# A hybrid decoder block on one core: the order of two of the seven products, and a fourth pair by seven products in the second part's down groups

## The chip, the cores and the metric

The kernel runs on one core of one Trainium2 chip. The metric is the device time of one execution in microseconds (us); lower is better. Before the change it is 1952.89 us, the median of three runs (1952.71 to 1953.48).

## What is computed

One decoder block with SEQ = 256 tokens, D_MODEL = 2048, D_FF = 5632, all in fp32:

```python
h = h + 0.5 * swiglu(rms_norm(h, ffn1_norm[i]), ffn1_w_gu[i], ffn1_w_down[i])
h = h + hybrid_mixer(rms_norm(h, mix_norm[i]), w_in[i], ...)
h = h + 0.5 * swiglu(rms_norm(h, ffn2_norm[i]), ffn2_w_gu[i], ffn2_w_down[i])
gate = jax.nn.sigmoid(rms_norm(h, ple_norm[i]) @ ple_w_gate[i])
h = h + gate * (p[i] @ ple_w_proj[i])
...
def swiglu(x, w_gu, w_down):
    gate, up = jnp.split(x @ w_gu, 2, axis=-1)
    return (jax.nn.silu(gate) * up) @ w_down
```

The change lies in the two SwiGLUs ("ffn 1" and "ffn 2"). The mixer between them and the gate behind them are not touched.

## The kernel before

**Precision.** Every fp32 operand of a matrix product is split into a high and a low part (`hi`, a rounding cast on ScalarE, ACT; `lo = x - hi`, a subtraction on VectorE, DVE), and a product takes three matmuls of TensorE (PE): hi times hi, hi times lo, lo times hi. One matmul has a 128x128 stationary side (activations) and a 128x512 moving side (weights).

**Groups.** A SwiGLU has 11 column blocks of 512 in its gate and up matrices, cut into three parts of 3, 4 and 4 blocks (`PARTS`, line 28). For each block there is a group `gu` (four banks of PSUM: gate and up, `g` and `u`, for two token tiles each), and behind the blocks of a part there are two groups `dn` for the down product of that part, with 1024 of the 2048 output columns each (four banks `d`). The groups of part 1 (the second part) of ffn 1 are the four `gu` groups from about 219 to 374 us and the two `dn` groups from 374 to 466 us; in ffn 2 they end at 1614 us.

**Pairs and products.** A group's inner dimension comes in pairs, of 256 rows each. A pair done the plain way is loaded as 512 KB for each of the two column blocks (`raw`), split by `weight_pair` (lines 74 and 75: `whi`, `wlo`, three buffers each) and multiplied by 12 matmuls (lines 540 to 542). So a pair takes 24 matmuls for both column blocks. The first `ns` pairs of a group go another way, by the scheme of Strassen and Winograd: the weights are cut into four quarters, loaded as tiles `R` (128 x 512 `ns`), and seven products of combined quarters with combined left sides give the four banks, at 3 matmuls for each pair and product: 21 instead of 24 for each pair. `NS` = 4 pairs in a `gu` group; `NS_DOWN` (line 32) = 2, 3, 3 pairs in the `dn` groups of the three parts.

**The seven products** (`Group.all_sums`, `halved` and `product`, lines 281 to 349). For each product the sum of quarters standing in `R` is split into `shi` (line 295, ACT) and `slo` (line 296, DVE), two buffers each; behind the first products DVE adds other quarters onto `R` (line 304), or GpSimd's queue (POOL) loads a quarter once more with an adding DMA (line 311). The products go into the banks c21, c12, c21, c21, c11, c12, c21 in this order. Behind the first two ACT copies the bank to c11 and c22 (line 344). Behind the third and the fourth ACT copies c21 into a tile `part` (line 347), which DVE subtracts from c12, and from c22 (line 349). The fourth product adds to c21, as the third, so it may start only when the copy of line 347 behind the third is through.

**The left sides** (`halves`, lines 425 to 462). For two pairs at a time DVE adds hi and lo of the activations into a tile `S` (line 452), makes four differences in it (line 458), ACT casts it to `Sh` (line 460), and DVE makes `Sl` (line 461). Products 0, 4 and 6 (counted from 0) take the activations themselves as left side; the others take `Sh` and `Sl`.

**The order.** While a group's plain pairs run, the seven products of the following group are put between them, one behind each plain pair from the first or the third on, and the rest behind the last (`plan`, the list `at`); the loads of the quarters of the group after that are put behind products 4 to 6, into the places that the follower's quarters leave (`loads`). This program order is then moved about by the framework's scheduler, engine by engine, so that a product's matmuls can stand scattered between those of plain pairs. Each engine works its own list strictly in order.

**The last block of a part.** `down_input` (line 477 on) makes `hTh` and `hTl`, the left side of the down product, of a block: two products on DVE, a transposition by 32x32 blocks, DMAs out and in, a cast and a subtraction. The plain pairs of the first `dn` group that use the last block are put last.

Of the kernel before, what the change touches and what calls it, by code (L numbers as in the profile page):

```python
# [10 lines left out]
F32 = mybir.dt.float32  # L11
# [16 lines left out]


NS = 4  # L30
NS_DOWN = tuple(3 if i1 - i0 == 4 else 2 for i0, i1 in PARTS)


W_IN_ORDER = (2, 0, 4, 3, 1, 5, 8, 10, 12, 9, 11, 13, 6, 7)
# [9 lines left out]
def block_kernel(ctx, tc, a, out):  # L44
# [200 lines left out]
    class Group:  # L245
# [32 lines left out]
        def loads(self, last=None):  # L278


            free = [last.home[q] for q in ((0, 1), (1, 0), (1, 1), (0, 0))] if last else ["R0", "R1", "R2", "R3"]
            self.queue = nc.gpsimd if last else nc.sync
            use = (0, 0), (0, 1), (1, 1), (1, 0)
            self.home = dict(zip(use, free))
            return [("load", lambda q=q: self.load(*q)) for q in use]

        def all_sums(self):

            fp = current[0]

            def halved(j, b):
                w = self.raw[j, b]
                hi = fp.tile([P, NS, NB], F32R, tag="shi", name="shi", bufs=2)[:, 0:self.ns]
                lo = fp.tile([P, NS, NB], F32R, tag="slo", name="slo", bufs=2)[:, 0:self.ns]
                keep(nc.scalar.copy(hi, w))  # L295
                nc.vector.tensor_tensor(out=lo, in0=w, in1=hi, op=ALU.subtract)  # L296
                return hi, lo

            def keep(ins):

                return tc.keep_in_program_order(ins) if self.first == "2" else ins

            def add(x, y):
                keep(nc.vector.tensor_tensor(out=self.raw[x], in0=self.raw[x], in1=self.raw[y], op=ALU.add))  # L304

            def add_loaded(x, y):


                if self.first:
                    return add(x, y)  # L310
                nc.gpsimd.dma_start(out=self.raw[x], in_=self.quarters[y[1]][y[0]], accum_op=ALU.add)

            for i, q in enumerate(((0, 0), (0, 0), (0, 0), (0, 1), (1, 0), (1, 1), (0, 0))):
                ws = halved(*q)
                if i == 0:
                    add((0, 0), (0, 1))
                    add_loaded((0, 1), (1, 1))
                elif i == 1:
                    add((0, 0), (1, 1))
                elif i == 2:  # L320
                    add_loaded((0, 0), (1, 0))
                yield ws
# [97 lines left out]
    def halves(kind, his, los, ns, wait=0):  # L420


        for _ in range(wait):
            yield
        fp = current[0]

        sh = fp.tile([P, NS, 2, 2, P], F32R, tag="Sh", name="Sh")
        sl = fp.tile([P, NS, 2, 2, P], F32R, tag="Sl", name="Sl")

        def side(i, g):  # L430
            if i in (0, 4, 6):
                k, t = 2 * (g % 2) + (i > 0), i // 6
                c = slice(t * P, (t + 1) * P)
                return his[g // 2][:, k, c], los[g // 2][:, k, c]
            j, t = {1: (1, 1), 2: (0, 0), 3: (0, 1), 5: (1, 0)}[i]
            return sh[:, g, j, t, :], sl[:, g, j, t, :]

        sides[kind] = side

        for g0 in range(0, ns, 2):  # L440
            n = min(2, ns - g0)
            hi, lo = his[g0 // 2], los[g0 // 2]
            keep = lambda ins: ins
            if g0 and n == 1:

                keep = tc.keep_in_program_order
                yield
            if n == 2:
                x = fp.tile([P, 2 * NB], F32, tag="sil", name="S")
            else:  # L450
                x = act.tile([P, NB], F32, tag="nat", name="S", bufs=4)
            keep(nc.vector.tensor_tensor(out=x, in0=hi[:, 0:2 * n].bitcast(F32).rearrange("p k x -> p (k x)"),
                                         in1=lo[:, 0:2 * n].bitcast(F32).rearrange("p k x -> p (k x)"), op=ALU.add))
            xv = x.rearrange("p (g j t y) -> p g j t y", g=n, j=2, t=2)
            a11, a12, a21, a22 = (xv[:, :, j, t, :] for t in range(2) for j in range(2))
            for o, y, z, op in ((a22, a21, a22, ALU.subtract), (a21, a11, a21, ALU.subtract),
                                (a11, a22, a11, ALU.subtract), (a12, a11, a12, ALU.add)):
                nc.vector.tensor_tensor(out=o, in0=y, in1=z, op=op)
            sx = [y[:, g0:g0 + n].rearrange("p g j t y -> p (g j t y)") for y in (sh, sl)]
            nc.scalar.copy(sx[0], x)  # L460
            nc.vector.tensor_tensor(out=sx[1], in0=x, in1=sx[0], op=ALU.subtract)
            yield

    def ffn(n, nT, r, scale, next_norm, stat):
        xs = picker(*nT)
        late = callable(r)
        with tc.tile_pool(name="ffn", bufs=1) as fp:
# [43 lines left out]
            for group, todo in ffn_plan[n]:  # L511
# [14 lines left out]
                    group.new_banks()  # L526
                for kind, one in todo:
                    if kind == "seventh":
                        group.follower.product(one)
                        continue  # L530
                    b, g = one
                    whi, wlo = next_weights()
# [29 lines left out]
                    else:  # L562
# [7 lines left out]
                        hTl.append(tl)  # L570
                        i0, i1 = PARTS[group.part]

                        last = (3 if i1 - i0 == 4 else 2) if len(hTh) == i1 else 0
                        gen = down_input(outs, sil, th, tl, last)
                        next(gen)

# [801 lines left out]
```

## Time and profile before

| | |
|---|---|
| median of three runs | 1952.89 us (1952.71 to 1953.48) |
| the profiled execution, its own time | 1953.25 us |
| its span in the trace | 1951.5 us |
| PE busy | 1932.7 us, 99% of the span, 8884 matmuls |
| weight loads of PE (beside the matmuls) | 1591.6 us, 82% |
| DVE busy | 1567.9 us, 80% |
| ACT busy | 1163.1 us, 60% |
| POOL busy | 148.8 us, 8% |
| granted clock of TensorE | 0.998 |
| chain that ended last | PE 87%, DVE 6%, DMA 4%, issue 2%, ACT 1% |

A matmul's busy time (0.39 us) is longer than the distance from one start to the next (0.23 us), since matmuls are pipelined; so 99% busy says only that PE seldom stands still. What a matmul costs is the distance of starts. The span is 1.75 us shorter than the execution's own time, which has the launch around it.

### The profile page before, as it was taken

The page shows a single profiled execution, that of the slowest core. Times are in us where ns is not written, and L with a number is a line of the kernel's source. Part 1 is how long each engine was busy: PE and PEld are TensorE (multiplying, and loading weights), DVE is VectorE, ACT ScalarE, POOL GpSimd, SP SyncE. Part 2 cuts the span into 40 slices and gives each one's busy share as a digit, 9 for nine tenths or more (in the row PEclk, how much of TensorE's full clock was granted, in tenths as well). Part 3 has the DMA queues.
Part 4 walks back from the last instruction along what each step waited for, and adds up shares of the span by engine and source line. Part 5 has one row for each costly group of instructions (what it writes and reads, how often), then busy time and mean ns, then how long its engine had stood idle before and what let it go on. Part 6 is the DMA issues. An engine that isn't in the chain of part 4 may idle for free.

```text
span 1951.5 us, 24163 instructions
## 1 busy us (share of the span) xinstructions
PE 1932.7 (99%) x8884; PEld 1591.6 (82%) x8884; DVE 1567.9 (80%) x1679; ACT 1163.1 (60%) x1358; POOL 148.8 (8%) x226
## 2 busy tenths in 40 slices
PE   9999999999999999999999999999999999999997
PEld 7888888888888888878788888888888788887886
DVE  7889878997889766797856579889888987888965
ACT  6656666566665567664555456566565755656653
POOL 0010100000010000010100000010000100001000
PEclk9999999999999999999999999999999999999999
DMA  8778888788887765556565786888898987988864
GB/s 311 268 238 276 255 288 285 227 293 251 282 283 237 225 216 172 175 169 209 173 201 160 244 289 226 226 285 289 241 282 251 303 266 237 272 255 282 249 208 141
DMA packets 144184, 475.06 MB, mean 243 GB/s; under 512 B 19649, under 2 KB 47297, under 8 KB 129857
## 3 DMA queue, kind: packets, MB, share of 16 engines
q1 hardware_dynamic: 107200, 302.16, 44.4%
q0 software_dynamic: 25920, 160.44, 30.2%
q10 hardware_dynamic: 10944, 10.91, 1.7%
q8 instruction: 69, 1.13, 0.2%
q14 instruction: 51, 0.41, 0.1%
HBM read 451.44 MB, written 22.02 MB: 243 GB/s over the span
## 4 chain that ended last, share of the span: by engine, by line
PE 87%; DVE 6%; DMA 4%; issue 2%; ACT 1%; SPq 0%; POOL 0%; POOLq 0%; DVEq 0%; ACTq 0%
PE g L340 5%; PE d L541 5%; PE d L542 5%; PE g L339 5%; PE d L540 4%; PE g L341 4%; PE u L540 4%; PE u L542 4%; PE u L541 4%; PE g L541 4%; PE g L542 4%; PE pj L109 4%; PE pj L110 4%; PE pj L111 4%; PE g L540 4%
## 5 line engine op out<-in xcount | busy, mean ns | idle before, releaser
L74 ACT CAST whi<-raw 128x1024 fp32r<-128x1024 f32 (+1 forms) x489 | 512.1, 1050 | 427.1 <-PE pj L111 109.9
L75 DVE TENSOR_TENSOR wlo<-raw,whi 128x1024 fp32r<-128x1024 f32 (+1 forms) x489 | 592.0, 1217 | 166.1 <-ACT whi L74 163.8
L296 DVE TENSOR_TENSOR slo<-R,shi 128x2048 fp32r<-128x2048 f32 (+2 forms) x224 | 445.2, 1989 | 149.0 <-ACT shi L295 147.6
L295 ACT CAST shi<-R 128x2048 fp32r<-128x2048 f32 (+2 forms) x224 | 374.2, 1671 | 140.5 <-DVE R L304 62.1
L109 PE MATMUL pj<-whi,nTh 128*128 128x512 f32 x448 | 179.4, 401 | 0.0
L110 PE MATMUL pj<-wlo,nTh 128*128 128x512 f32 x448 | 175.3, 391 | 1.1 <-DVE wlo L75 1.1
L111 PE MATMUL pj<-whi,nTl 128*128 128x512 f32 x448 | 174.9, 390 | 0.0
L541 PE MATMUL d<-wlo,hTh 128*128 128x512 f32 x448 | 174.3, 389 | 0.0
L540 PE MATMUL d<-whi,hTh 128*128 128x512 f32 x448 | 174.2, 389 | 0.0
L542 PE MATMUL d<-whi,hTl 128*128 128x512 f32 x448 | 173.7, 389 | 0.0
L541 PE MATMUL g<-wlo,nTh 128*128 128x512 f32 x400 | 155.9, 390 | 0.4 <-DVE wlo L75 0.4
L541 PE MATMUL u<-wlo,nTh 128*128 128x512 f32 x400 | 155.7, 389 | 0.5 <-DVE wlo L75 0.5
L542 PE MATMUL g<-whi,nTl 128*128 128x512 f32 x400 | 155.8, 390 | 0.0
L542 PE MATMUL u<-whi,nTl 128*128 128x512 f32 x400 | 155.7, 389 | 0.0
L540 PE MATMUL g<-whi,nTh 128*128 128x512 f32 x400 | 155.4, 390 | 0.0
L540 PE MATMUL u<-whi,nTh 128*128 128x512 f32 x400 | 154.2, 389 | 0.2 <-ACT whi L74 0.2
L304 DVE TENSOR_TENSOR R<-R 128x2048 f32<-128x2048 f32 (+2 forms) x68 | 135.7, 1995 | 0.1
L110 PEld LDWEIGHTS pj<-wlo,nTh 128*128 128x128 f32 x448 | 84.2, 188 | 18.9 <-DVE wlo L75 2.7
L111 PEld LDWEIGHTS pj<-whi,nTl 128*128 128x128 f32 x448 | 84.1, 188 | 17.6
L542 PEld LDWEIGHTS d<-whi,hTl 128*128 128x128 f32 x448 | 84.1, 188 | 17.6
L541 PEld LDWEIGHTS d<-wlo,hTh 128*128 128x128 f32 x448 | 84.1, 188 | 17.6
L540 PEld LDWEIGHTS d<-whi,hTh 128*128 128x128 f32 x448 | 84.1, 188 | 17.4
(332 smaller groups left out, 3445.2 us busy)
## 6 DMA issues: line engine op xcount, KB each, us to landing
raw<-in_w_gu SPq DMA_DIRECT2D x199, 512.0 KB, 5.7
raw<-in_w_down SPq DMA_DIRECT2D x112, 512.0 KB, 6.5
raw<-in_w_in SPq DMA_DIRECT2D x112, 512.0 KB, 3.4
R<-in_w_gu2q POOLq DMA_DIRECT2D x54, 1024.0 KB, 8.6
R<-in_w_gu1q POOLq DMA_DIRECT2D x48, 1024.0 KB, 8.6
raw<-in_w_out SPq DMA_DIRECT2D x32, 512.0 KB, 4.2
tT<-scr SPq DMA_DIRECT2D x22, 512.0 KB, 5.1
R<-in_w_down11q POOLq DMA_DIRECT2D x12, 768.0 KB, 6.0
```

Source lines behind the costliest of these rows:

```text
L74: nc.scalar.copy(hi[:, j, :], raw[:, j, :])
L75: nc.vector.tensor_tensor(out=lo[:, j, :], in0=raw[:, j, :], in1=hi[:, j, :], op=ALU.subtract)
L109: nc.tensor.matmul(outs[t], xh[:, c], whi[:, j, :], start=st, stop=False)
L110: nc.tensor.matmul(outs[t], xh[:, c], wlo[:, j, :], start=False, stop=False)
L111: nc.tensor.matmul(outs[t], xl[:, c], whi[:, j, :], start=False, stop=sp)
L295: keep(nc.scalar.copy(hi, w))
L296: nc.vector.tensor_tensor(out=lo, in0=w, in1=hi, op=ALU.subtract)
L304: keep(nc.vector.tensor_tensor(out=self.raw[x], in0=self.raw[x], in1=self.raw[y], op=ALU.add))
L339: nc.tensor.matmul(out, xh, whi[:, g, :], start=st, stop=False, skip_group_check=True)
L540: nc.tensor.matmul(out, xh[:, c], whi[:, j, :], start=st, stop=False, skip_group_check=True)
L541: nc.tensor.matmul(out, xh[:, c], wlo[:, j, :], start=False, stop=False, skip_group_check=True)
L542: nc.tensor.matmul(out, xl[:, c], whi[:, j, :], start=False, stop=sp, skip_group_check=True)
```

## The change

Five things are edited; all else stays.

1. `NS_DOWN` becomes (2, 4, 3): the two `dn` groups of the second part take four instead of three pairs by seven products, in both SwiGLUs. Their quarters grow from 128x1536 to 128x2048, and they have four instead of five plain pairs for each column block.
2. `SEVEN` puts product 4 (into c11) in front of product 3 (into c21), in the loads' splits and in the products.
3. `loads` gives the freed tiles of quarters on in the order in which they now come free.
4. `halves` makes the left sides of four pairs of a `dn` group in three steps: pairs 0 and 1 together, pair 2 and pair 3 in tiles of one pair each (128x512, of the pool's `nat`), and doesn't hand over to other work between the last two.
5. `last`, the number of steps for which the last block's cast is put off, is 2 instead of 3 in the second part.

```diff
-NS_DOWN = tuple(3 if i1 - i0 == 4 else 2 for i0, i1 in PARTS)
+NS_DOWN = (2, 4, 3)
+SEVEN = (0, 1, 2, 4, 3, 5, 6)
...
-            free = [last.home[q] for q in ((0, 1), (1, 0), (1, 1), (0, 0))] if last else ["R0", "R1", "R2", "R3"]
+            free = [last.home[q] for q in ((1, 0), (0, 1), (1, 1), (0, 0))] if last else ["R0", "R1", "R2", "R3"]
...
-            for i, q in enumerate(((0, 0), (0, 0), (0, 0), (0, 1), (1, 0), (1, 1), (0, 0))):
-                ws = halved(*q)
+            for i in SEVEN:
+                ws = halved(*((0, 0), (0, 0), (0, 0), (0, 1), (1, 0), (1, 1), (0, 0))[i])
...
-        for g0 in range(0, ns, 2):
-            n = min(2, ns - g0)
-            hi, lo = his[g0 // 2], los[g0 // 2]
+        for g0, n in {1: ((0, 1),), 2: ((0, 2),), 3: ((0, 2), (2, 1)),
+                      4: ((0, 2), (2, 1), (3, 1)) if kind == "dn" else ((0, 2), (2, 2))}[ns]:
+            k0 = 2 * (g0 % 2)
+            hi, lo = (x[g0 // 2][:, k0:k0 + 2 * n] for x in (his, los))
...
-            if g0 and n == 1:
+            if g0 >= 2 and n == 1:
 
                 keep = tc.keep_in_program_order
-                yield
+                if g0 == 2:
+                    yield
...
-            yield
+            if g0 + n != 3 or ns == 3:
+                yield
...
-                        group.follower.product(one)
+                        group.follower.product(SEVEN[one])
...
-                        last = (3 if i1 - i0 == 4 else 2) if len(hTh) == i1 else 0
+                        last = (6 - NS_DOWN[group.part] if i1 - i0 == 4 else 2) if len(hTh) == i1 else 0
```

The lists of the engines show where the work comes to stand. A name's number tells one buffer from another; `d1_1308` is a bank, `shi_1318` with `slo_1319` the split weights of one product. Line numbers of the change are 3 to 6 higher.

**PE, first part of ffn 1, from the end of product 2 on** (the second `dn` group's products between the first one's plain pairs). Before:

```order
L339 MATMUL d1_1308<-shi_1318,Sh_1008 128x512
L340 MATMUL d1_1308<-slo_1319,Sh_1008 128x512
L341 MATMUL d1_1308<-shi_1318,Sl_1009 128x512
L339 MATMUL d1_1308<-shi_1348,Sh_1008 128x512
L340 MATMUL d1_1308<-slo_1349,Sh_1008 128x512
L341 MATMUL d1_1308<-shi_1348,Sl_1009 128x512
```

The change:

```order
L342 MATMUL d1_1308<-shi_1318,Sh_1008 128x512
L343 MATMUL d1_1308<-slo_1319,Sh_1008 128x512
L344 MATMUL d1_1308<-shi_1318,Sl_1009 128x512
L342 MATMUL d0_1307<-shi_1348,hTh_520 128x512
L343 MATMUL d0_1307<-slo_1349,hTh_520 128x512
L344 MATMUL d0_1307<-shi_1348,hTl_521 128x512
```

Before, the next product goes into the same bank `d1_1308`; now it is product 4, into another bank and with the activations as left side.

**ACT, second part of ffn 1, end of the last `gu` group: the casts of the first `dn` group's products 3 to 6.** Before:

```order
L344 COPY d1_2791<-d0_2790 128x512
L295 CAST shi_2838<-R_2587 128x1536
L347 COPY part_2869<-d1_2789 128x512
L295 CAST shi_2872<-R_2633 128x1536
L74 CAST whi_2952<-raw_2951 128x1024
L499 CAST hTh_2677<-tT_2896 128x4x4x32 x2
L347 COPY part_2907<-d1_2789 128x512
L295 CAST shi_2910<-R_2625 128x1536
L74 CAST whi_3001<-raw_3000 128x1024
L295 CAST shi_2935<-R_2548 128x1536
```

The change:

```order
L347 COPY d1_2799<-d0_2798 128x512
L298 CAST shi_2852<-R_2633 128x2048
L350 COPY part_2886<-d1_2797 128x512
L298 CAST shi_2889<-R_2584 128x2048
L77 CAST whi_2975<-raw_2974 128x1024
L505 CAST hTh_2677<-tT_2913 128x4x4x32 x2
L77 CAST whi_3027<-raw_3026 128x1024
L298 CAST shi_2927<-R_2625 128x2048
L350 COPY part_2955<-d1_2797 128x512
L298 CAST shi_2958<-R_2548 128x2048
```

The second copy to `part` stands behind the third cast instead of in front of it, and the four casts are a third wider.

**DVE, second part of ffn 1, first `dn` group: from the left side of the third block to the third product's `slo`** of the second `dn` group. Before:

```order
L500 TENSOR_TENSOR hTl_2678<-tT_2896,hTh_2677 128x4x4x32 x2
L296 TENSOR_TENSOR slo_2995<-R_2876,shi_2994 128x1536
L482 STREAM_TRANSPOSE tb_2977<-sil_2825 128x4x128 x2
L304 TENSOR_TENSOR R_2876<-R_2876,R_2939 128x1536
L75 TENSOR_TENSOR wlo_3002<-raw_3000,whi_3001 128x1024
L75 TENSOR_TENSOR wlo_3034<-raw_3032,whi_3033 128x1024
L296 TENSOR_TENSOR slo_3016<-R_2876,shi_3015 128x1536
L75 TENSOR_TENSOR wlo_3073<-raw_3071,whi_3072 128x1024
L304 TENSOR_TENSOR R_2876<-R_2876,R_2941 128x1536
L75 TENSOR_TENSOR wlo_3105<-raw_3103,whi_3104 128x1024
L452 TENSOR_TENSOR S_3334<-nTh_99,nTl_103 128x1024
L296 TENSOR_TENSOR slo_3067<-R_2876,shi_3066 128x1536
```

The change (the row of `hTl_2678` and one `wlo` stand in front, as they are):

```order
L488 STREAM_TRANSPOSE tb_3000<-sil_2836 128x4x128 x2
L299 TENSOR_TENSOR slo_3021<-R_2893,shi_3020 128x2048
L457 TENSOR_TENSOR S_3348<-nTh_99,nTl_103 128x1024
L307 TENSOR_TENSOR R_2893<-R_2893,R_2962 128x2048
L78 TENSOR_TENSOR wlo_3063<-raw_3061,whi_3062 128x1024
L78 TENSOR_TENSOR wlo_3105<-raw_3103,whi_3104 128x1024
L299 TENSOR_TENSOR slo_3045<-R_2893,shi_3044 128x2048
L463 TENSOR_TENSOR S_3348<-S_3348 128x2x128
L307 TENSOR_TENSOR R_2893<-R_2893,R_2964 128x2048
L78 TENSOR_TENSOR wlo_3140<-raw_3138,whi_3139 128x1024
L463 TENSOR_TENSOR S_3348<-S_3348 128x2x128 x3
L299 TENSOR_TENSOR slo_3099<-R_2893,shi_3098 128x2048
```

Three subtractions and two sums are a third wider, and the four differences of the next `gu` groups' left side (`S_3348`) have come in front of the last row.

## Rows read from the trace of the kernel before

**Rows 1.** The page, busy times: engine, us (share of the span), instructions.
```profile
PE 1932.7 (99%) x8884; PEld 1591.6 (82%) x8884; DVE 1567.9 (80%) x1679; ACT 1163.1 (60%) x1358; POOL 148.8 (8%) x226
```

**Rows 2.** Windows: stretch, length, busy us (instructions) of each engine, clock, DMA share, GB/s.
```profile
219.00:341.00 122.00, 122.00 (x540) 100.86 (x539) 100.10 (x70) 75.22 (x67) 11.95 (x18) 1.00 0.87 270
```

**Rows 3.** Timeline of PE, its waits for `part`: start, us, instruction [idle before <-releaser].
```profile
160.36 0.39 PE L341 MATMUL d<-shi,Sl 128*128 128x512 f32 x1
161.43 0.50 PE L339 MATMUL d<-shi,Sh 128*128 128x512 f32 x1 [0.68 <-ACT part L347]
161.76 0.39 PE L340 MATMUL d<-slo,Sh 128*128 128x512 f32 x1
...
646.77 0.50 PE L339 MATMUL d<-shi,Sh 128*128 128x512 f32 x1 [0.73 <-ACT part L347]
...
1308.00 0.50 PE L339 MATMUL d<-shi,Sh 128*128 128x512 f32 x1 [0.68 <-ACT part L347]
...
1545.81 0.50 PE L339 MATMUL d<-shi,Sh 128*128 128x512 f32 x1 [0.64 <-ACT part L347]
```

**Rows 4.** Windows in the second part of ffn 1, columns as in rows 2.
```profile
337.60:354.30 16.70, 16.70 (x75) 13.84 (x74) 16.55 (x19) 5.71 (x7) 0.89 (x1) 1.00 0.70 209
374.20:395.30 21.10, 21.10 (x94) 17.34 (x94) 21.10 (x19) 13.17 (x12) 1.97 (x3) 1.00 0.88 272
```

**Rows 5.** Groups of instructions by form: line, engine, form, count | busy, mean ns | idle.
```profile
L296 DVE TENSOR_TENSOR slo<-R,shi 128x2048 fp32r<-128x2048 f32 x133 | 304.4, 2289 | 116.4 <-ACT shi L295 115.6 <-DMA raw<-in_w_gu 0.6
L295 ACT CAST shi<-R 128x2048 fp32r<-128x2048 f32 x133 | 254.5, 1914 | 108.8 <-DVE R L304 53.7 <-PE g L341 31.0 <-PE u L341 18.3
L296 DVE TENSOR_TENSOR slo<-R,shi 128x1536 fp32r<-128x1536 f32 x56 | 98.2, 1755 | 22.7 <-ACT shi L295 22.3
L304 DVE TENSOR_TENSOR R<-R 128x2048 f32<-128x2048 f32 x42 | 95.7, 2278 | 0.1
L295 ACT CAST shi<-R 128x1536 fp32r<-128x1536 f32 x56 | 83.0, 1483 | 16.8 <-PE d L341 10.7 <-PE u L341 2.5 <-DMA R<-in_w_down21q 2.1
L458 DVE TENSOR_TENSOR S<-S 128x256 f32<-128x256 f32 x76 | 31.9, 420 | 0.9
L304 DVE TENSOR_TENSOR R<-R 128x1536 f32<-128x1536 f32 x16 | 27.9, 1742 | 0.0
```

**Rows 6.** Timeline, second part of ffn 1: the last `gu` group's first `u` pair.
```profile
337.68 1.76 DVE L296 TENSOR_TENSOR slo<-R,shi 128x1536 fp32r<-128x1536 f32 x1 [1.58 <-ACT shi L295]
353.06 1.22 DVE L75 TENSOR_TENSOR wlo<-raw,whi 128x1024 fp32r<-128x1024 f32 x1
355.23 0.39 PE L541 MATMUL u<-wlo,nTh 128*128 128x512 f32 x1
```

**Rows 7.** Timeline, the same place: products 3 to 6 behind the last `gu` pairs.
```profile
365.80 0.63 PE L341 MATMUL d<-shi,Sl 128*128 128x512 f32 x2
368.57 1.49 ACT L295 CAST shi<-R 128x1536 fp32r<-128x1536 f32 x1
371.77 0.39 PE L341 MATMUL d<-shi,Sl 128*128 128x512 f32 x1
372.19 0.59 ACT L347 COPY part<-d 128x512 f32<-128x512 f32 x1
375.87 0.75 DVE L477 SCALAR_TENSOR_TENSOR sil<-u,rstd,sil 128x512 f32<-128x512 f32 x1
376.17 0.40 PE L340 MATMUL d<-slo,Sh 128*128 128x512 f32 x1
```

**Rows 8.** Timeline, the first `dn` group: the third product's `slo` (first of two), and its use.
```profile
393.60 3.42 DVE L296 TENSOR_TENSOR slo<-R,shi 128x1536 fp32r<-128x1536 f32 x2
395.70 0.39 PE L340 MATMUL d<-slo,Sh 128*128 128x512 f32 x1
```

**Rows 9.** DMA issues of quarters: out<-in, queue, count, KB each, median us to landing.
```profile
R<-in_w_gu2q POOLq DMA_DIRECT2D x54, 1024.0 KB, 8.6
R<-in_w_down11q POOLq DMA_DIRECT2D x12, 768.0 KB, 6.0
```

More of the change, by code (lines that the diff above doesn't have):

```diff
@@ L451, in halves @@
                 x = act.tile([P, NB], F32, tag="nat", name="S", bufs=4)
-            keep(nc.vector.tensor_tensor(out=x, in0=hi[:, 0:2 * n].bitcast(F32).rearrange("p k x -> p (k x)"),
-                                         in1=lo[:, 0:2 * n].bitcast(F32).rearrange("p k x -> p (k x)"), op=ALU.add))
+            keep(nc.vector.tensor_tensor(out=x, in0=hi.bitcast(F32).rearrange("p k x -> p (k x)"),
+                                         in1=lo.bitcast(F32).rearrange("p k x -> p (k x)"), op=ALU.add))
             xv = x.rearrange("p (g j t y) -> p g j t y", g=n, j=2, t=2)
```

## The prediction

> **What bounds the kernel now.** I read the page's busy times first: PE is busy for 99% of the span, DVE for 80%, ACT for 60% [rows 1]. So the time is the number of PE's matmuls times their distance, plus the moments in which PE stands still. The distance is read from a stretch where PE never waits: 540 matmuls in 122 us, 0.226 us each [rows 2]. Next I looked for the moments: in the waits of PE the longest are four for the copy of line 347 [rows 3]. Last I asked who is close to making PE wait. In the second part of ffn 1 the windows show DVE busy for 16.55 of 16.70 us and then for 21.10 of 21.10 us [rows 4], while PE doesn't wait: DVE delivers there just in time. Any DVE work added in these windows has no idle time to go into.
>
> **Part by part.** The sum is made against the profiled execution, 1953.25 us, which is 0.36 above the median of the runs.
>
> *A. Matmuls.* A pair by seven products takes 21 matmuls instead of 24. One pair more in two groups of each SwiGLU: 4 x 3 = 12 matmuls fewer. At 0.226 us [rows 2]: **-2.7 us**. PE is the bound, so this counts in full.
>
> *B. Product 4 in front of product 3.* Product 3 adds to c21 and must wait for the copy of c21 behind product 2. At 161.43 it stands right behind it: 1.07 us from start to start instead of 0.23, and the next start comes after 0.33 instead of 0.23, so 0.95 us are lost. The other three waits, with idle times of 0.73, 0.68 and 0.64 beside 0.68 here, lose about as much [rows 3]: 3.8 us together. In the change product 4, which goes into another bank, stands between; its 6 or 9 matmuls (1.4 to 2.0 us) are longer than the wait. What is late next: product 6 needs c21 after the copy behind product 3, but product 5 lies between, so this costs nothing; with two products on end, 0.9 us at most. Between 0 and -3.8 I take **-3.8 us**, since the cover is longer than each wait.
>
> *C. DVE and ACT in the second part.* A split of 128x2048 costs DVE 2289 instead of 1755 ns (+0.53) and ACT 1914 instead of 1483 (+0.43); a sum of quarters 2278 instead of 1742 (+0.54) [rows 5]. Three places of ffn 1 follow in PE's list; ffn 2 has the same three in the same order.
>
> *C1, the first `u` pair of the last `gu` group.* Its `wlo` is ready at 354.28 and used at 355.23: 0.95 to spare, with DVE without a gap since the `slo` of 337.68, which itself had waited for its cast [rows 6]. Ahead of this `wlo` now stand two wider `slo` and two wider sums (2.14) and one wider cast (0.43): 2.57 later. PE comes to it one matmul (0.23) later. 2.57 - 0.95 - 0.23 = 1.4.
>
> *C2, products 3 to 6 of the first `dn` group.* Before, plain matmuls lie between them; in PE's list of the change they stand nearly end to end, 12 matmuls each. `shi` and `slo` have two buffers, so a cast starts only when the last product but one is through. Products 1 and 2 end at 365.80 and just behind; the second cast after them ends at 370.06, 4.26 later [rows 7]. With two wider casts: 5.12. PE's list has 17 matmul distances there, 3.8 us: 1.3 lost. The next link took 4.40 us, from the last matmul of 371.77 to the `slo` used at 376.17, with a copy to `part` (0.59) in the cast's way, which the change moves back [rows 7]. 4.40 + 0.43 + 0.53 - 0.59 = 4.8, with 15 distances, 3.4: 1.4 lost. Together 2.7.
>
> *C3, the third product in the first `dn` group.* Its `slo` is ready at 395.35 and used at 395.70: 0.35 to spare [rows 8]. In the lists shown DVE has ahead of it three wider `slo` (1.60), two wider sums (1.07) and the four differences of the next left side (4 x 0.42 = 1.68 [rows 5]), but no longer one product of `sil` (0.75 [rows 7]): 3.6 more. PE comes to it 6 matmuls (1.4) later. 3.6 - 0.35 - 1.4 = 1.9.
>
> C is 1.4 + 2.7 + 1.9 = 6.0 for each SwiGLU, **+12.0 us**. Once PE has lost it, it can't be made up, as PE has no idle time. Bounds: nothing, if the lists fall so that PE always finds something else, as it does today; above, all DVE work added up to the middle of the first `dn` group without cover. That is 7 x 0.53 + 2 x 0.54 = 4.8 for each of two groups, less two `wlo` of 1.22 [rows 6], plus 2.1 for the small tiles (an estimate: half of four differences [rows 5] and of two 128x1024 operations [rows 6]): 9.3 for each SwiGLU, 18.6. I take 12.0, because each of the three places is worked out from its own slack.
>
> *Costed at nothing.* The left side of pair 3 (edit 4) goes into DVE's time while PE has `u` pairs; without that cover it is the 2.1 in the upper bound. Edits 3 and 5 move loads and one cast: the last block is now needed two plain pairs earlier, 24 matmuls or 5.4 us, of which the delays C2 and C3 give back 4.6; at worst 0.8 for each SwiGLU. The bytes of the weights stay, save for the adding loads, which grow with the quarters; how late they can be is a rival below.
>
> **Sum:** 1953.25 - 2.7 - 3.8 + 12.0 = 1958.75, against the median **1958.4 us**, 0.28% slower. What a measurement of this kernel can tell from no change is 0.2%, 3.9 us: slower means over 1956.8, faster under 1949.0.
>
> **The rivals.**
>
> *Faster: DVE's delays stay hidden.* For it: today DVE is just as full and PE loses next to nothing, as its list has plain matmuls ready at the right moments. Against it: in the change's list products 3 to 6 stand end to end, with six plain matmuls between them in all. It decides at the link of C2: if a `slo` follows within 12 matmuls (2.7 us) of its buffer's release, nothing is lost; it takes 4.4 now. Time: 1953.25 - 6.5 - 0.36 = 1946.4. Chance 0.09.
>
> *No difference: half of C.* If the wait of C1 gives DVE enough of a lead, C2 or C3 shrinks; if C3 falls away (1.9 twice) the time is 1954.6, with C1 gone too 1951.8. Against it: DVE has no gap for the 21 us behind products 5 and 6, so a lead would have to come from PE's waits in C2 alone. Chance 0.31.
>
> *Slower still: quarters land late.* Loads of 768 KB land after 6.0 us, of 1024 KB after 8.6 [rows 9]; 2.6 later in the four groups, if nothing covers it, is +10.4. The tiles come free one product earlier relative to their use, with wider products between, so I take a third of it, +3.5: 1961.9. [...] Chance 0.10.
>
> That the change doesn't do what it says is out: PE's list is 12 matmuls shorter.
>
> **Numbers.** The forecast has 0.50, with 1955.5 to 1961 as its own range; the rivals 0.09, 0.31 and 0.10. Faster 0.09, same 0.31, slower 0.60. The range reaches into "half of C" and up to the late quarters with some of C's upper bound: 1951.5 to 1963.5 leaves out the faster rival and the last tenth above.
>
> **What the profile after would show.** A: 8872 matmuls. B: no wait of PE for the copy to `part` in `dn` groups. C: in the second part of both SwiGLUs, waits of PE for `wlo` in the first `u` pair of about 1.4 us, for the cast and the subtraction of products 3 and 5 of about 1.3 each, for the third product of the next group of about 1.9; and no such waits in the first and third part. The prediction is wrong if PE keeps the 0.226 us distance through the second part (then faster), or if its waits there are for landings of `R` (then slower for another reason).

## The result: 0.3% slower, and where the profile shows it

After the change the kernel takes 1958.0 us (median of 10 runs, 1957.5 to 1959.3), against 1952.6 (1950.8 to 1953.5) for the kernel before, timed beside it: a ratio of 1.0032, 95% interval 1.0024 to 1.0040. The profiled execution of the changed kernel took 1957.71 us, its span is 1956.0.

The page's busy times, answering to [rows 1]: 12 matmuls fewer, DVE 16.4 us more.

```profile
PE 1929.7 (99%) x8872; PEld 1589.9 (81%) x8872; DVE 1584.3 (81%) x1683; ACT 1168.8 (60%) x1352; POOL 148.4 (8%) x226
```

Windows, the first over the same work as [rows 2], the others over those of [rows 4]; columns as there. Where PE doesn't wait, nothing has changed: 540 matmuls in 122 us. In the second part PE is no longer busy throughout (19.48 of 21.10), and DVE still has next to no idle time.

```profile
219.40:341.40 122.00, 122.00 (x540) 100.99 (x539) 99.95 (x70) 75.54 (x67) 11.91 (x18) 1.00 0.88 279
337.60:354.30 16.70, 16.70 (x75) 13.82 (x74) 16.67 (x15) 5.65 (x6) 0.89 (x1) 1.00 0.71 199
374.20:395.30 21.10, 19.48 (x84) 15.62 (x85) 20.95 (x19) 12.65 (x12) 3.08 (x5) 1.00 0.79 275
```

The waits of PE by releaser (us in total, times, longest) show the exchange. The wait for `part` is gone from the list, and three others stand at its top. In each SwiGLU two waits are for a cast (`shi`), one large one for a subtraction (`slo`) and one for a `wlo`.

```profile
PE d L342 <- ACT shi L298: 5.5, 4, 1.7
PE d L343 <- DVE slo L299: 3.0, 4, 1.3
PE u L547 <- DVE wlo L78: 2.6, 2, 1.3
```

Their places in ffn 1, from PE's timeline (start, us, instruction, idle before). The first two rows are the place of [rows 3]: product 4 starts 0.23 us behind product 2 instead of 1.07. The third row holds two matmuls; the second of them starts at 354.75.

```profile
160.72 0.39 PE L344 MATMUL d<-shi,Sl 128*128 128x512 f32 x1
160.95 0.39 PE L342 MATMUL d<-shi,hTh 128*128 128x512 f32 x1
...
354.53 0.61 PE L546 MATMUL u<-whi,nTh 128*128 128x512 f32 x2
356.42 0.50 PE L547 MATMUL u<-wlo,nTh 128*128 128x512 f32 x1 [1.28 <-DVE wlo L78]
...
373.04 0.40 PE L548 MATMUL u<-whi,nTl 128*128 128x512 f32 x1
374.52 0.50 PE L342 MATMUL d<-shi,Sh 128*128 128x512 f32 x1 [1.08 <-ACT shi L298]
...
380.34 0.39 PE L547 MATMUL d<-wlo,hTh 128*128 128x512 f32 x1
382.02 0.50 PE L343 MATMUL d<-slo,Sh 128*128 128x512 f32 x1 [1.29 <-DVE slo L299]
...
403.39 0.39 PE L342 MATMUL d<-shi,Sh 128*128 128x512 f32 x1
405.46 0.50 PE L342 MATMUL d<-shi,hTh 128*128 128x512 f32 x1 [1.68 <-ACT shi L298]
```

From start to start the four waits take 1.67, 1.48, 1.68 and 2.07 us, so 1.44, 1.25, 1.45 and 1.84 more than a matmul's 0.23, and behind each comes one distance of 0.34, 0.11 more. That is 6.4 us for ffn 1, and ffn 2 has the same four (1505.73, 1523.85, 1531.35 and 1554.79).

A sum over everything is a better measure: all that PE's distances from start to start have over 0.227 us, in a stretch. From 340 to 420 us (second part of ffn 1) it was 1.1 and is 7.3; from 1490 to 1570 us (ffn 2) it was 2.0, of which 1.0 is one wait for `part`, and is 7.4. So C costs 6.3 in each, 12.6 together. Outside these, the other three waits for `part` and some small ones beside them give 3.1. A last wait, in the gate behind ffn 2 (for a `wlo`, at 1929 us), was there before and is gone: 1.0, which no part of the prediction speaks of. With 2.7 for the matmuls, 12.6 - 1.0 - 3.1 - 1.0 - 2.7 = 4.8 from PE's first to its last matmul, and the spans differ by 4.5.

The same sum for the kernels below, with their times:

| kernel | second part, ffn 1 | ffn 2 | median, us |
|---|---|---|---|
| before | 1.1 | 2.0 | 1952.6 |
| the change | 7.3 | 7.4 | 1958.0 |
| new order, three pairs | 1.2 | 1.2 | 1948.3 |
| four pairs, old order | 10.0 | 10.3 | 1967.7 |
| narrower sums | 8.0 | 7.5 | 1958.3 |
| both groups a pair earlier | 4.5 | 4.5 | 1953.7 |
| second group a pair earlier | 11.5 | 11.8 | 1966.1 |
| edit 4 undone | 7.5 | 7.5 | 1958.2 |
| next sums held in order | 6.7 | 6.7 | 1960.0 |
| both earlier, a sum on GpSimd | 14.4 | 13.0 | 1969.1 |
| both earlier, narrower sums | 4.0 | 4.0 | 1951.1 |
| three pairs, a pair earlier | 0.1 | 0.1 | 1946.7 |

### The profile page after: what moved, and what is told of

Same layout as the page of the kernel before. It is cut to its first block, busy times and chain, and to the rows that moved or that the text cites. A ratio compares the mean times of both kernels' runs of the same rounds, so it can differ in the third digit from the quotient of the medians.

```text
span 1956.0 us, 24082 instructions
## 1 busy us (share of the span) xinstructions
PE 1929.7 (99%) x8872; PEld 1589.9 (81%) x8872; DVE 1584.3 (81%) x1683; ACT 1168.8 (60%) x1352; POOL 148.4 (8%) x226
## 4 chain that ended last, share of the span: by engine, by line
PE 86%; DVE 8%; issue 2%; DMA 2%; ACT 1%; POOL 0%; SPq 0%; DVEq 0%; POOLq 0%; ACTq 0%
PE d L548 4%; PE d L546 4%; PE g L343 4%; PE d L547 4%; PE g L342 4%; PE g L344 4%; PE u L547 4%; PE u L548 4%; PE u L546 4%; PE pj L112 4%; PE pj L113 4%; PE pj L114 4%; PE g L547 4%; PE g L548 4%; PE g L546 4%
## 5 line engine op out<-in xcount | busy, mean ns | idle before, releaser
L77 ACT CAST whi<-raw 128x1024 fp32r<-128x1024 f32 (+1 forms) x481 | 503.7, 1050 | 422.1 <-PE pj L114 108.8
L78 DVE TENSOR_TENSOR wlo<-raw,whi 128x1024 fp32r<-128x1024 f32 (+1 forms) x481 | 582.8, 1218 | 160.3 <-ACT whi L77 159.1
L299 DVE TENSOR_TENSOR slo<-R,shi 128x2048 fp32r<-128x2048 f32 (+2 forms) x224 | 459.8, 2055 | 133.3 <-ACT shi L298 131.9
L298 ACT CAST shi<-R 128x2048 fp32r<-128x2048 f32 (+2 forms) x224 | 385.8, 1724 | 128.6 <-DVE R L307 61.0
L546 PE MATMUL d<-whi,hTh 128*128 128x512 f32 x416 | 162.1, 390 | 0.0
L547 PE MATMUL d<-wlo,hTh 128*128 128x512 f32 x416 | 161.9, 389 | 0.0
L548 PE MATMUL d<-whi,hTl 128*128 128x512 f32 x416 | 161.2, 389 | 0.0
L112 PEld LDWEIGHTS pj<-whi,nTh 128*128 128x128 f32 x448 | 84.2, 188 | 16.7
L546 PEld LDWEIGHTS d<-whi,hTh 128*128 128x128 f32 x416 | 78.1, 188 | 17.1 <-ACT hTh L505 1.0
L548 PEld LDWEIGHTS d<-whi,hTl 128*128 128x128 f32 x416 | 78.1, 188 | 16.5
```

The source lines that it names most:

```text
L77: nc.scalar.copy(hi[:, j, :], raw[:, j, :])
L78: nc.vector.tensor_tensor(out=lo[:, j, :], in0=raw[:, j, :], in1=hi[:, j, :], op=ALU.subtract)
L112: nc.tensor.matmul(outs[t], xh[:, c], whi[:, j, :], start=st, stop=False)
L546: nc.tensor.matmul(out, xh[:, c], whi[:, j, :], start=st, stop=False, skip_group_check=True)
L547: nc.tensor.matmul(out, xh[:, c], wlo[:, j, :], start=False, stop=False, skip_group_check=True)
L548: nc.tensor.matmul(out, xl[:, c], whi[:, j, :], start=False, stop=sp, skip_group_check=True)
```

## The experiments

Each stands against the changed kernel (1958.0 us) and was timed beside the kernel before, whose median was 1951.6 to 1952.2 in these comparisons. Beside the changed kernel it was 1952.6, so a difference of less than 1 us to 1958.0 says nothing.

### The order without the fourth pair, and the fourth pair without the order

```diff
-NS_DOWN = (2, 4, 3)
+NS_DOWN = (2, 3, 3)
```

> The new order of the products with the old three pairs: part B alone, so 12 matmuls more than the changed kernel and no wider quarters. My theory (parts A, B and C add up: -2.7, -3.8 and +12.0 against the kernel before): the four waits of PE for the copy to part are gone, none of the waits of about 1.4 to 1.9 us in the second part comes in their place, and the time is the median before less 3.8, 1948.8 us, a ratio of 0.998. First rival, product 4 in front of product 3 has a price of its own (its quarters are wanted one product earlier, or DVE's subtraction behind the copy comes late for product 5): the time stays within 1 us of the kernel before, or above it. Second rival, the waits of the second part come from the order and not from the fourth pair: they are seen here too, at 355 to 405 us and at 1505 to 1555 us, and the time is above 1955.

Measured: 1948.25 us, ratio 0.9982 (0.9973 to 0.9991). B is worth 3.7 us where 3.8 was worked out (the interval is 1.8 to 5.3, so the agreement to 0.1 is closer than the measurement). Without the fourth pair PE loses at most 0.4 us at any place of the second parts, and neither rival holds.

```diff
-SEVEN = (0, 1, 2, 4, 3, 5, 6)
+SEVEN = (0, 1, 2, 3, 4, 5, 6)
...
-            free = [last.home[q] for q in ((1, 0), (0, 1), (1, 1), (0, 0))] ...
+            free = [last.home[q] for q in ((0, 1), (1, 0), (1, 1), (0, 0))] ...
```

> The fourth pair with its small tiles, and the products in their old order: parts A and C without B. My theory: the four waits for the copy to part (0.95 us lost at each) are back and the waits of the second part stay, so 1958.0 + 3.8 = 1961.8 us, a ratio of 1.0047 to the kernel before. In the second part two of the copies stand among waits that are there anyway, so somewhat less may come back: down to 1959.9. Rival, the new order is what makes PE wait in the second part: without it the waits of 1.3 to 1.9 us at 374, 382 and 405 us are gone or shorter than 0.5, and the time is 1953 or below.

Measured: 1967.65 us, ratio 1.0079 (1.0066 to 1.0091), 6 us over what I expected. The waits for `part` are back (0.8 to 1.0 each). The `wlo` (1.44 lost) and two waits at the places of C2 (1.23 and 1.06, the second now for a cast) stay as well, so the fourth pair brings them and not the order. But at the place of C3 stands a longer wait, for another thing. Waits of PE by releaser, and the timeline of that place:

```profile
PE d L546 <- ACT hTh L505: 5.6, 2, 2.9
PE d L342 <- ACT shi L298: 4.0, 4, 1.1
PE d L342 <- ACT part L350: 2.9, 4, 0.8
```

```profile
397.08 0.33 SPq L499 DMA_DIRECT2D tT<-scr  x1
...
403.90 0.39 PE L548 MATMUL d<-whi,hTl 128*128 128x512 f32 x1
406.30 0.62 ACT L505 CAST hTh<-tT 128x512 fp32r<-128x512 f32 x1 [2.99 <-DMA tT<-scr]
406.97 0.50 PE L546 MATMUL d<-whi,hTh 128*128 128x512 f32 x1 [2.69 <-ACT hTh L505]
```

PE has run out of products and stands before the plain pairs of the part's last block, whose load `tT` was issued at 397.08 and landed 9.2 us later. In the changed kernel this load is issued at 396.92 and the cast starts at 406.43, just as late; there PE is held up by C3 until 405.46, has products left, and comes to the first plain pair with that block at 408.35. So in the changed kernel the wait of C3, together with the products left behind it, covers the block's lateness.

Windows of the same run (length, busy us (count) of PE, PEld, DVE, ACT, POOL, then PEclk, DMA share, GB/s) show what it costs beside the wait: the granted clock falls behind it.

```profile
402.00:404.00 2.00, 2.00 (x11) 1.55 (x9) 1.97 (x3) 0.57 (x1) 0.00 (x0) 1.00 0.92 242
404.00:407.00 3.00, 0.32 (x3) 0.03 (x1) 0.17 (x2) 0.70 (x2) 0.00 (x0) 1.00 0.98 401
408.00:412.00 4.00, 4.00 (x12) 3.09 (x11) 3.67 (x3) 3.99 (x4) 0.65 (x1) 0.57 0.00 0
412.00:425.00 13.00, 13.00 (x59) 10.76 (x58) 12.21 (x11) 8.60 (x7) 1.89 (x4) 1.00 0.94 286
```

Before the wait the clock is 1.00 with 11 matmuls in 2 us. From 408 to 412 the mean is 0.57, with 12 in 4 us. The lengthened distances behind the wait add up to 1.9 us. So the 9.6 us by which the span is longer than the changed kernel's come out: 2.7 and 2.9 in the second parts, and 4.0 outside them, where the waits for `part` are back.

### Is it DVE's backlog, or the chain of cast and subtraction?

In this kernel DVE leaves out the last 512 columns of the two sums of quarters of the four-pair groups, so those products' weights are not the full sums.

```diff
+                s = slice(0, min(3, self.ns) if self.kind == "dn" else self.ns)
-                keep(nc.vector.tensor_tensor(out=self.raw[x], in0=self.raw[x], in1=self.raw[y], op=ALU.add))
+                keep(nc.vector.tensor_tensor(out=self.raw[x][:, s], in0=self.raw[x][:, s], in1=self.raw[y][:, s], op=ALU.add))
```

> The changed kernel, in which DVE's two sums of quarters of the down groups with four pairs leave out their last 512 columns: 1742 instead of 2278 ns for each of four sums of a SwiGLU, while casts and subtractions stay wide. It tells whether DVE's backlog or the chain of cast and subtraction sets each wait. My theory: C1 (the wlo at 356 us) and C3 (the third product at 405) hang on DVE's backlog and fall by about 1.07 each, from 1.44 to about 0.4 and from 1.84 to about 0.8; C2 (the cast at 374 and the subtraction at 382) hangs on the release of the two buffers and on the chain behind it, and stays at 1.25 and 1.45 within 0.3, unless PE's shorter wait at 356 brings it there earlier, in which case it grows. Time: 1958.0 - 2 x 2 x 1.05 = 1953.8 us, a ratio of 1.0006. First rival, DVE's backlog sets all of them: the two of C2 fall too, and the time is 1951 or below. Second rival, nothing of it is DVE's backlog (C1 and C3 are chains of releases as well): the waits stay, and the time is 1957 or above.

Measured: 1958.28 us, ratio 1.0032 (1.0020 to 1.0043): no gain at all. By its time the second rival would hold, but the places speak against it. PE's timeline, and the third product's cast, first here and then in the changed kernel:

```profile
354.50 0.50 PE L343 MATMUL d<-shi,Sh 128*128 128x512 f32 x1 [0.16 <-ACT Sh L466]
...
373.12 0.50 PE L343 MATMUL d<-shi,hTh 128*128 128x512 f32 x1 [1.78 <-ACT shi L298]
375.40 0.50 PE L343 MATMUL d<-shi,Sh 128*128 128x512 f32 x1 [1.77 <-ACT shi L298]
...
405.31 0.50 PE L343 MATMUL d<-shi,hTh 128*128 128x512 f32 x1 [0.70 <-ACT shi L298]
```

```profile
401.03 1.91 ACT L298 CAST shi<-R 128x2048 fp32r<-128x2048 f32 x1 [0.99 <-DVE R L308]
```

```profile
401.19 1.91 ACT L298 CAST shi<-R 128x2048 fp32r<-128x2048 f32 x1 [2.01 <-DVE R L307]
```

C1 falls from 1.44 to 0.32 (the first row, where PE now waits for the left side rather than the `wlo`), by about the 1.07 taken off DVE: it is DVE's backlog. C3 falls from 1.84 to 0.86, but mostly because PE comes there 0.8 us later than in the changed kernel. Its cast starts only 0.16 earlier, in both kernels behind DVE's sum of quarters: DVE sets this wait, but that it falls by the work taken off is not shown. C2 doesn't shrink but grows, to 1.95 and 2.05, now one matmul apart. My reading is that PE comes earlier to products on end, whose casts still wait for one of two buffers. Behind this pair of waits the granted clock falls as above (0.52 from 376.0 to 379.4 us, with 10 matmuls in 3.4 us). So the 2.1 us of C1 and C3 come back as 1.3 of waiting and some 1.5 at the lower clock (in ffn 2 as 0.8 and 1.5). My expectation had the waits right by place and the time wrong: I had named growth of C2, but not priced it.

### Spreading the products

Here the products of both four-pair groups begin a plain pair earlier.

```diff
-                    1 if group.kind == follower.kind else 2
+                    (1 if group.kind == follower.kind else 2) - (follower.kind == "dn" and follower.ns == 4)
```

> The changed kernel, in which the seven products of the two down groups with four pairs begin one plain pair earlier in the group before, so that the last four of the first such group no longer stand end to end behind the last plain pair. My theory: C2 comes from products on end, with two buffers for the halves of their quarters; with plain matmuls between them the two waits of 1.25 and 1.45 us fall below 0.5 each, and C3, which begins one pair earlier as well, falls to about 0.5. C1 grows, as the wider work of DVE now stands ahead of one u pair more: from 1.44 to about 2.5. By DVE's and ACT's lists run through with the durations of the trace, each SwiGLU loses 4.8 us at its waits instead of 7.3: 1958.0 - 5.1 = 1952.9 us, a ratio of 1.0002. Rival, DVE has too much work in the stretch, wherever the products stand: what C2 and C3 lose, C1 gains, and the time stays within 1.5 us of 1958. Second rival, quarters that are asked for one pair earlier have not landed: PE waits on ACT's casts, which wait on landings, and the time is above 1959.

Measured: 1953.73 us, ratio 1.0007 (0.9999 to 1.0016), 4.3 less than the changed kernel. Both waits of C2 and that of C3 are below 0.2, and C1 is near what it was worked out to be:

```profile
357.55 0.50 PE L547 MATMUL u<-wlo,nTh 128*128 128x512 f32 x1 [2.18 <-DVE wlo L78]
```

2.57 us from start to start, 2.34 lost (behind this one the matmuls stay 0.23 us apart). So C2 goes when plain matmuls stand between the products (they also start earlier here, and the two are not told apart), and the work that is too much for DVE, 2.3 us, gathers at one place.

Then only the second group's products earlier, those of the first as in the changed kernel:

```diff
-                    1 if group.kind == follower.kind else 2
+                    (follower.ns < 4 or follower.kind == "gu") if group.kind == follower.kind else 2
```

> The changed kernel, in which the seven products of only the second of the two down groups with four pairs begin one plain pair earlier; those of the first stay. My theory: C1 and the first wait of C2 stay (1.44 and 1.25 us), and the second wait of C2 and C3, at which the second group's first products stand between the first group's last ones, fall below 0.3 each: 1958.0 - 2 x (1.2 + 1.7) = 1952.2 us, a ratio of 0.9998, and better than with both groups moved (1953.7), where C1 grew to 2.34. Rival, DVE's work in the stretch is too much by a fixed amount of some 2.5 us a SwiGLU: what falls behind 380 us comes back at one of the first two waits, and the time is that of both groups moved, 1953 to 1954.5.

Measured: 1966.06 us, ratio 1.0070 (1.0057 to 1.0082), 14 above my theory and 12 above the rival. The waits I spoke of went as expected: at 355.73 and 373.89 they stay (1.44 and 1.26 lost), at 381 0.2 is left and C3's is gone. In its place stands the wait that the kernel with the old order showed, for the last block:

```profile
403.90 1.14 ACT L505 CAST hTh<-tT 128x512 fp32r<-128x512 f32 x2 [6.29 <-DMA tT<-scr]
404.57 0.50 PE L546 MATMUL d<-whi,hTh 128*128 128x512 f32 x1 [2.69 <-ACT hTh L505]
407.40 0.80 PE L342 MATMUL d<-shi,Sh 128*128 128x512 f32 x1 [1.15 <-ACT shi L298]
```

with a second wait 3 us on, with matmuls that take 0.63 us or more instead of 0.39 from 405.1 us on, and a granted clock of 0.50 from 408 to 412. The load of `tT` was issued 3.6 us earlier (393.35 instead of 396.92), but took 10.5 us to land instead of 9.5. PE, having used up the products that cover it, came to the block 6.6 us earlier (401.7 instead of 408.35).

### Terms and edits on their own

Edit 4 undone:

```diff
-                      4: ((0, 2), (2, 1), (3, 1)) if kind == "dn" else ((0, 2), (2, 2))}[ns]:
+                      4: ((0, 2), (2, 2))}[ns]:
```

> The changed kernel with pairs 2 and 3 of the down groups' left side summed together in one large tile again (edit 4 undone). My theory: edit 4 was costed at nothing, since these sums go into DVE's time while PE has u pairs; without the small tiles the time stays within 1 us of 1958.0, with a little more lost at 360 us (0.5 a SwiGLU by the lists run through with the trace's durations). First rival, the small tiles are what lets the first product of the first down group start in time: without them PE loses up to half a large sum's chain more in each SwiGLU (2.1 us by the upper bound of C), 1962.2 us. Second rival, the small tiles cost DVE six instructions more a SwiGLU for nothing: the waits of the second part shrink and the time is 1956 or below.

Measured: 1958.18 us, ratio 1.0033 (1.0021 to 1.0044). No difference, as costed: 0.3 more at 361 and 363 us, 0.2 less at 374.

The sums of the next left side held in program order (`pin` is set for the `gu` side behind the second part):

```diff
-            keep = lambda ins: ins
+            keep = tc.keep_in_program_order if pin else lambda ins: ins
```

> The changed kernel with the sums and differences of the next gu group's left side, behind the second part, held in the order in which they are written instead of being moved ahead in DVE's list. It tests the term C3, in which I counted four differences (1.68 us) ahead of the third product of the second down group. My theory: the wait at 405 us falls from 1.84 to about 0.2, nothing comes in its place, and the time is 1958.0 - 2 x 1.65 = 1954.7 us. Rival, DVE's list has the same work in the stretch either way: the wait at 405 falls by about half and a wait of about 1.5 us comes back at 450 to 460 us, at the first products on the new left side; the time stays within 1 us of 1958.0. By the lists run through with the durations of the trace it is the rival (1.0 left at 403 and 1.5 new at 459 us).

Measured: 1959.97 us, ratio 1.0042 (1.0028 to 1.0056); the rival holds by its waits, with a time 2.0 above 1958.0 where it allowed 1. PE's timeline:

```profile
405.09 0.50 PE L342 MATMUL d<-shi,hTh 128*128 128x512 f32 x1 [0.90 <-ACT shi L298]
...
461.32 0.50 PE L342 MATMUL g<-shi,Sh 128*128 128x512 f32 x1 [1.32 <-ACT shi L298]
```

C3 falls by 0.8, not by 1.65, and 1.5 comes back at 461 us. The four differences ahead of the third product were a part of C3, but holding them back only moves the loss to a later place.

### Taking work off DVE with the products spread

Both groups a pair earlier, and one sum of each on GpSimd:

```diff
+                engine = nc.gpsimd if self.kind == "dn" and self.ns == 4 and y == (1, 1) else nc.vector
-                keep(nc.vector.tensor_tensor(out=self.raw[x], in0=self.raw[x], in1=self.raw[y], op=ALU.add))
+                keep(engine.tensor_tensor(out=self.raw[x], in0=self.raw[x], in1=self.raw[y], op=ALU.add))
```

> Both down groups with four pairs one plain pair earlier, and the second of the two sums of quarters that each needs done by GpSimd instead of DVE: 2 x 2278 ns of DVE's time less in the second part of each SwiGLU. It tells whether what is left with products one pair earlier (2.34 at 357 us and some 0.7 behind it) is DVE's backlog. My theory: it is, so with 2.28 less ahead of the wlo of the first u pair that wait falls to about 0.1 and the time is 1953.7 - 2 x 2.2 = 1949.3 us or less. No row of the trace shows GpSimd summing tiles of this size (its largest operation there is 0.56 us for 128x256); if it takes over 5 us for one, the third product, which reads the sum, waits for it, and the loads that GpSimd issues behind it start late. Rival, that: new waits of over 1 us for the third product's cast at about 365 and 395 us, and the time is 1954 or above.

Measured: 1969.07 us, ratio 1.0089 (1.0075 to 1.0102); the rival holds by its time, and for a reason beyond GpSimd's own 4.6 to 5.5 us. Its wait stands in the second group alone (at 406 us, where the third product's cast comes behind GpSimd's sum); in the first group PE waits for a `wlo`, at 352.6. The timeline of DVE and POOL, and the two waits:

```profile
346.68 1.30 DVE L489 STREAM_TRANSPOSE tb<-sil 128x512 f32<-128x512 f32 x2
346.85 4.60 POOL L308 TENSOR_TENSOR R<-R 128x2048 f32<-128x2048 f32 x1 [4.10 <-DVE slo L299]
347.90 4.63 DVE L78 TENSOR_TENSOR wlo<-raw,whi 128x1024 fp32r<-128x1024 f32 x1
...
398.65 5.48 POOL L308 TENSOR_TENSOR R<-R 128x2048 f32<-128x2048 f32 x1 [3.96 <-DVE slo L299]
399.63 6.16 DVE L464 TENSOR_TENSOR S<-S 128x256 f32<-128x256 f32 x4
```

```profile
352.58 0.50 PE L548 MATMUL g<-wlo,nTh 128*128 128x512 f32 x1 [1.61 <-DVE wlo L78]
...
404.16 1.90 ACT L298 CAST shi<-R 128x2048 fp32r<-128x2048 f32 x1 [6.33 <-POOL R L308]
406.11 0.80 PE L343 MATMUL d<-shi,Sh 128*128 128x512 f32 x1 [3.48 <-ACT shi L298]
```

A `wlo`, 1.22 us in the changed kernel, takes 4.63 and ends 1.08 behind GpSimd's sum of 4.60; the two transpositions beside the same sum take 1.30, as in the changed kernel (1.30 at 387.3 us). Beside the second sum, of 5.48, four differences take 6.16 where one takes 0.42. So nothing was taken off DVE (a sum of 2.28 went, 3.4 came at this `wlo`), and this run can't tell whether C1 is backlog. Why the one operation takes longer and the other not, no run shows. (In the kernel before, GpSimd's operation on the largest tile is a fill of 128x1024 in 0.96 us; the 0.56 of the expectation is not its largest.)

The cleaner test, with the narrower sums in place of GpSimd (the same columns left out as above):

> Both down groups with four pairs one plain pair earlier, and DVE's two sums of quarters of each without their last 512 columns: 1.07 us less of DVE's work in each group, with nothing moved to GpSimd. My theory: the wait of 2.34 us for the wlo at 357 is DVE's backlog and falls by 1.07 to about 1.3, the rest stays, and the time is 1953.7 - 2 x 1.07 = 1951.6 us; with the second group's 1.07 felt too, 1950. Rival, the last block of the hidden layer: PE comes to it a microsecond or two earlier, its load from DRAM has not landed, and PE waits for the cast hTh at about 403 us in place of the wlo; the time stays at 1953.7 or rises above it, up to 1966, if the wait is as long as in the run with the second group alone moved.

Measured: 1951.08 us, ratio 0.9996 (0.9987 to 1.0006), 2.65 less than with full sums, for 2 x 1.07 expected. C1 is DVE's backlog; it falls by 1.0 in each SwiGLU:

```profile
356.35 0.50 PE L548 MATMUL u<-wlo,nTh 128*128 128x512 f32 x1 [1.16 <-DVE wlo L78]
```

2.18 of idle time became 1.16. About half of that is lost again at 402 us, so the two second parts give 1.0 together, and the spans differ by 2.0. The theory reached the time, but only 1.0 of it at the place it named; the rest are small differences outside, about which it says nothing. This run also tells more of C2. It has the same narrower sums as the run above without the earlier start, and C1 differs by only 1.0 (1.32 and 0.32 lost), but the two waits of C2, 1.95 and 2.05 there, are 0.1 or less here: a wait 1.0 longer at C1 can't account for 4.0.

### A version that beats both

```diff
-NS_DOWN = (2, 4, 3)
+NS_DOWN = (2, 3, 3)
...
-                    1 if group.kind == follower.kind else 2
+                    (1 if group.kind == follower.kind else 2) - (follower.kind == "dn")
```

> The new order with three pairs, and the products of every down group's pairs begin one plain pair earlier. With three pairs PE still loses about 0.3 to 0.4 us at each of four slo (369, 377, 617 and 625 us) of each SwiGLU and 0.1 at the start behind each. My theory: with a plain pair more behind the products these go, no DVE work having been added: 8 x 0.45 = 3.6 us less than 1948.3, that is 1944.7 us, a ratio of 0.9965. Rival, as with four pairs the work only moves: the wlo of the first u pair comes late at 355 us or the last block of the hidden layer at 395 us, and the time is 1948 or above.

Measured: 1946.73 us, ratio 0.9972 (0.9962 to 0.9983) to the kernel before, 1.5 less than the new order alone and 2.0 more than expected; the spans differ by 2.0. The four `slo` waits of each SwiGLU are gone. In ffn 1 that is 2.0 us, 1.8 were expected. In ffn 2 nothing of it is kept. In the list of waits a new one stands first, in the gate behind the SwiGLU, where PE now arrives before its left side:

```profile
PE g L689 <- ACT nTh L161: 1.5, 1, 1.5
```

## Why the prediction held, point by point

The time (1958.4 predicted, 1958.0 measured) and the cause were right. That the time agrees to 0.4 us is in part luck: ten runs of one kernel spread over 1.8 to 2.7 us, and by the two traces C was 0.6 over its 12.0, while 1.0 was won at the wait in the gate, which was not foreseen and whose cause stays open, and some 0.3 at small waits.

- **A**, 12 matmuls at 0.226: they are gone, and the distance in the quiet stretch is the same. The -2.7 itself no run isolates.
- **B**, -3.8: right, shown by the waits that are gone and by the run of the order alone (-3.7). What came in its place is small, 0.1 us more of other waits in each second part.
- **C1**, 1.4: 1.44. It is DVE's backlog: with 1.07 less work it shrinks by 1.12 in one kernel and by 1.0 in another.
- **C2**, 1.3 and 1.4: 1.25 and 1.45, at the cast and at the subtraction named. With plain matmuls between the products and an earlier start both go.
- **C3**, 1.9: 1.84, in the place named. The link was drawn one step short: the sum of quarters ends late (DVE, 401.1), the third product's cast starts behind it at 401.19, the fourth's at 403.52, and PE, having put the fourth product between the third's matmuls, waits for the fourth's cast (405.46). The third's `slo` is ready some 0.2 behind that, so the size is the same.
- **C as a sum of three terms**, each with its own slack, and its bound "once PE has lost it, it can't be made up": it gave the size for this list of instructions, but the terms are not separate prices. Taking one away feeds another: less at C1 made C2 grow by 1.3, and the earlier start that removed C2 and C3 left 2.3 at C1.
- **Edit 4 at nothing**: shown. **Edits 3 and 5 at nothing**, "at worst 0.8 for each SwiGLU": PE doesn't wait for the last block in this kernel, since the delays of C3 help to cover it, as the text had it; no run undoes either edit by itself. Where they don't cover it, the block costs 2.8 us of waiting or more and some 2 at the lower clock, not 0.8. That is the price I had most wrong, and it made two of my expectations for experiments miss by 6 and 14 us.
- **The rivals.** "All hidden" and "half of C" needed a lead for DVE, and the changed kernel's lists give none; nearly half of C goes only where the products start earlier (1953.7). "Quarters land late": they did land later where they are wider, and neither PE nor a cast of ACT waited for one in the changed kernel.

The landings, to [rows 9]:

```profile
R<-in_w_gu2q POOLq DMA_DIRECT2D x54, 1024.0 KB, 8.4
R<-in_w_down11q POOLq DMA_DIRECT2D x12, 1024.0 KB, 7.3
```

7.3 us for the wider quarters instead of 6.0: 1.3 later, half of the 2.6 that this rival took.

What stays open: whether four pairs can be had without loss. Two limits stand against it, DVE's 2.3 us too many in each second part and the last block's load; the best version seen with four pairs and full sums takes 1953.7, 5.5 us over three pairs with the new order. A third buffer for `shi` and `slo` was not tried.

## What to carry to other kernels

Where the bound engine has 99% and the next one fills a stretch to the last tenth, a change that saves work on the first by adding to the second has to be costed in that stretch, by each consumer's slack there, and not by the shares of the whole span. Such slacks are a shared account: an experiment that removes one wait should name in advance the wait that will take it over, and a wait may be the only cover of a transfer that is later still. Two halves of a change can have opposite signs: here the reordering gave 3.7 us, and the fourth pair took 9.8 on top of it and 15.7 without it, so time them apart and together.

## What was not expected of the hardware

A pause of PE in the middle of the kernel cost more than itself in some of these runs. Behind 2.69 us of idle time (old order) the granted clock was 0.57 on average from 408 to 412 us, and behind two of 1.78 and 1.77 one matmul apart (narrower sums) 0.52 from 376.0 to 379.4; the lengthened distances come to 1.9 and some 1.5 us. In the run with the second group alone moved it was 0.50 from 408 to 412, behind 2.69 and a second wait of 1.15. In the run with a sum on GpSimd, behind 3.48, the matmuls are 0.43 us apart instead of 0.23 (406.70 to 408.84). Behind 2.18 (products a pair earlier) they stay 0.23 apart, and at the same place of ffn 2 the clock is 1.00 from 1505 to 1509; it is 1.00 too behind the 1.1 to 1.7 of the changed kernel. And the sum moved from DVE to GpSimd gave DVE no time: beside its 4.60 us a `wlo` took 4.63 instead of 1.22, 3.4 more.
